# First FFN's second product: the order of the next layer's leading weights, the tails and the first steps' splits

## The chip, the cores and the metric

The kernel runs on one core of a Trainium2 chip, as one launch. The metric is the device time of one execution in microseconds (us), the median of several executions. Engines are named as in the profile: PE is TensorE, DVE is VectorE, ACT is ScalarE, POOL is GpSimd, and SP is the engine that sends nearly all DMAs.

## The reference

Two layers (DEPTH = 2) work on 512 tokens of width 1024. Layer 0 mixes tokens by a short gated convolution, layer 1 by a Mamba-2 scan; behind each mixer stands a SwiGLU feed-forward network (FFN) with an inner width of 2816. Around each of the four sub-layers stand two RMS norms and a shift, scale and gate that come from a conditioning vector:

```python
h = rmsnorm(x, norm_g[i, 2]) * (1.0 + scale) + shift
gate_, up = jnp.split(h @ f_w_in[i], 2, axis=-1)
y = (jax.nn.silu(gate_) * up) @ f_w_out[i]
x = x + gate * rmsnorm(y, norm_g[i, 3])
...
h = rmsnorm(x, norm_g[i, 0]) * (1.0 + scale) + shift    # next layer
z, xbc, dt_raw = jnp.split(h @ m_w_in, ..., axis=-1)
```

The change is in layer 0's FFN, at the product with `f_w_out[0]`, and in the passage from there to the first product of layer 1, with `m_w_in`. All of it is float32.

## The kernel before

**Split operands.** A float32 matrix product is made of three TensorE products. Each operand is split into a high part (a cast on ScalarE) and a low part (a subtraction on VectorE); `split_w` does this for weights. So each weight tile costs a DMA, one ScalarE and one VectorE instruction, in this order, before TensorE can use it.

**The second product.** The product with `f_w_out[0]` is computed over the first 16 of 22 blocks of the inner width by a Strassen scheme with seven products on quarter matrices (`PRODUCTS`: banks A to D, weights b11 to b22, activations a11 to s1). The list `seq` holds its 28 steps of 12 matmuls ("s") and four plain steps ("p") for blocks 16 and 17 of both column halves and 18 and 19 of half 0; the steps are numbered q = 0 to 31. `w_prep(item)` splits a step's weights, `a_prep(item)` its activations (and updates the raw activations for later products). In the loop, the program of step q holds the product, then `behind(q)` (copies of finished banks, and sums of weight quarters), then `w_prep` of step q + 4 and `a_prep` of step q + 3. The loop of the first product, ahead of it, already splits steps 0 and 1 within its last two tiles. Between the two loops stand the gating of the last inner block (`up(NF - 1, ...)`), the low parts that are still due (`low_parts`), two gate rows and step 2's and step 3's splits.

**Gate rows.** `put_gates(s)` turns a column of gate values into a row: a transpose on TensorE, then (second step of the generator) a copy on VectorE into the tile `gr`, of which there is one, and a DMA on SP to `gate_d`. Rows 2 and 3 are made here; they are read in layer 1.

**Weight rows.** `y_load` brings six tiles of the right half of `f_w_out[0]` (`w2y`) into the places of the activations `h`, which the last tile of the first product reads; two more are in staging buffers (`w4`, `w2s`). `add_` sends sums of weight quarters as accumulating DMAs on Pool.

**Tails and leading weights.** What is left is kept for the end (`tails`: three pieces of two blocks, one for column half 0 and two for half 1), so that the row tiles of 128 tokens end one after the other. Their raw weights are loaded into `xns`, tiles that later take the normalized rows, and that lie where `wx` lay. For the first product of layer 1, six weight tiles are prepared ahead (`ssd_lead`: three loads of 256 columns, `load_lead`; the first has 32 columns of dt and a memset behind them). Each load goes to one of two staging buffers `wst`; the four splits of a load are put into the list `lead_ops`, and the buffer is free for the next but one load when they are done. Load 2 so takes load 0's buffer.

**The boundary.** `finish(tail_w, leads)` runs the order in the string `BOUNDARY`, written out by hand: for each row tile t, the tail's matmuls (m0_t for column half 0, m1a_t and m1b_t for half 1), the bank's sum with the held product and its square (sq0_t, sq1_t; line 432 and 433), the gate (yg, 439), the new x (x, 456), its square (xs, 475) and root (rt3, 485), the normalized row (xn, 493 and 495). Then follow the transposes of row tiles 0 and 1 (tr0_p, line 502), for each block j of h the value (u), the high (hi) and the low part (lo; lines 511 to 520), and the first six tiles of layer 1's product in pieces by k (k0_k for tokens 0 to 255, k1_k for the rest).

Within these parts the order on TensorE, ScalarE, VectorE, SP and Pool is the program's (`manual_schedule`); each engine works through its instructions in order, and each waits for its operands.

Of the kernel before, what the change touches and what calls it, by code (L numbers as in the profile page):

```python
# [9 lines left out]
F32R = mybir.dt.float32r  # L10
# [6 lines left out]
P = 128  # L17
T = 512
# [20 lines left out]
def trunk_kernel(  # L39
# [17 lines left out]
    whl_p = ctx.enter_context(tc.tile_pool(name="whl", bufs=4))  # L57
# [147 lines left out]
    def split_w(src, dst, nk):  # L205
        act.copy(dst[:, 0, :nk, :], src)
        dve.tensor_tensor(dst[:, 1, :nk, :], src, dst[:, 0, :nk, :].bitcast(F32), SUB)
# [102 lines left out]
    def put_gates(s, bank=aux_ps):  # L310

        pt = bank("ggp")
        pe.transpose(pt[:KD, :P], gcol[:, s * KD:(s + 1) * KD], ident)
        yield
        gr = tmp.tile([KD, P], F32, tag="gr", name="gr", bufs=1)
        dve.tensor_copy(gr, pt[:KD, :P])
        dma(gate_d[s], gr)
        yield
# [261 lines left out]
    with ExitStack() as ph:  # L580
# [113 lines left out]
        with tc.manual_schedule(engines={PE_ENGINE, mybir.EngineType.SP, mybir.EngineType.Activation,  # L694
# [7 lines left out]
            load = lead_load(0, 1)  # L702
# [207 lines left out]
            for k in range(18):  # L910
                i, jp = k % 6, 2 + k // 6 * 2
# [65 lines left out]
        def tile4l(shape, dtype, name):  # L977
            return lead_p[0].tile(shape, dtype, tag="b", name=name)
# [30 lines left out]
        def up(f, pst):  # L1009
            g = gates[f]  # L1010
            if f < NS:
                dve.tensor_mul(raw[f // 4][:, f % 4, :], pst, g)
                if f % 4 == 3:
                    p = f // 2 - 1
                    lows.append(lambda: dve.tensor_tensor(a_("s1", p, 2), a_("a21", p, 2), a_("a22", p, 2), SUB))
                    lows.append(lambda: dve.tensor_tensor(a_("a21", p, 2), a_("a11", p, 2), a_("a21", p, 2), SUB))
                return
            a = acts[f] = ffp.tile([P, 2, T], F32R, tag="a", name=f"ff{f}")
            dve.tensor_mul(g, pst, g)
            act.copy(a[:, 0, :], g)  # L1020
            lows.append(lambda: dve.tensor_tensor(a[:, 1, :], g, a[:, 0, :].bitcast(F32), SUB))

        def low_parts():
            while lows:
                lows.pop(0)()
# [75 lines left out]
        def a_prep(item):  # L1101
            if item[0] == "p":
                return
            a = a_of[item] = ao_p[0].tile([P, 2, 2, 256], F32R, tag="ao", name="ao")
            (i, p), _ = tiles_s[item[1]]
            src = a_(PRODUCTS[i][2], p, 2)
            act.copy(a[:, 0], src)
            dve.tensor_tensor(a[:, 1], src, a[:, 0].bitcast(F32), SUB)
            if i == 0:
                dve.tensor_tensor(a_("a11", p, 2), a_("s1", p, 2), a_("a11", p, 2), SUB)  # L1110
            elif i == 1:
                dve.tensor_add(a_("a12", p, 2), a_("a12", p, 2), a_("a11", p, 2))
# [39 lines left out]
        with tc.manual_schedule(engines={PE_ENGINE, mybir.EngineType.SP, mybir.EngineType.Activation,  # L1152
                                         mybir.EngineType.DVE, mybir.EngineType.Pool}):
            load_pair(0)
            madds = ada_begin(14)
            for i, f in ((0, 0), (2, 0), (1, 1), (3, 1), (4, 2), (5, 3)):
                rest(i)
                if i in (2, 3):
                    up(f, lead_ps[i])
                    sums(1)  # L1160
                    low_parts()
                else:
                    gate(f, lead_ps[i])
                sums(1)
            finish = out_begin(1, w2, lambda k: acts[k], NF, ggs, xn_lead, "aux", None,
                               lambda: load_w([(wm_in, P, P)]), ys=ys, held=held)[2]
            plain_tiles = finish(())
            tiles = []
            last = 2 * NF - 7
            for k in range(last + 1):  # L1170
                if k % 2 == 0 and k < 2 * NF - 10:
                    load_pair(k // 2 + 1)
                if k in (16, 20, 24):
                    x_load((k - 16) // 4)
                if k in (last - 2, last - 1):
                    xy_load(n_s - 2 + k - last + 2)
                tiles.append(in_chunk(ws[k], h))
                for step in todo:
                    next(step, None)
                q, j = divmod(k - 3, 4)  # L1180
                if j < 2 and k > 2:
                    gate(4 + 2 * q + j, tiles[k - 1])
                elif k:
                    up(2 + 2 * q + j, tiles[k - 1])
                if k + 2 < len(splits):
                    for op in splits[k + 2]:
                        op()
                low_parts()
                sums(4 if j < 2 else 3)
                if k == 2 * NF - 12:  # L1190
                    ggs.append(make_gg(1, gg_tile))
                if k == last - 1:
                    assert next(madds, None) is None and not ada_sets and not quarters
                    sums_p.close()
                    ph.enter_context(tc.tile_pool(name="gap", bufs=1, side="right", reuse_waits="tile")).tile(
                        [P, 216], F32, tag="gap", name="gap")
                    ao_p.append(ph.enter_context(tc.tile_pool(name="aop", bufs=3, side="right", reuse_waits="tile")))
                    ao_p[0].tile([P, 2, 2, 256], F32R, tag="ao", name="ao")
                    gotp = ph.enter_context(tc.tile_pool(name="gotp", bufs=1, side="right", reuse_waits="tile"))
                    c22 = gotp.tile([P, 2, T], F32, tag="c22", name="c22")  # L1200
                if k >= last - 1:
                    w_prep(seq[k - last + 1])
                    a_prep(seq[k - last + 1])
            up(NF - 1, tiles[-1])
            low_parts()
            for step in todo:
                list(step)
            for q in (2, 3):
                list(put_gates(q, mm_ps))
            for p in range(n_s - 2):  # L1210
                y_load(p)
            for p in range(n_s):
                add_(b_("b12", p), b_("b11", p))
            w_prep(seq[2])
            w_prep(seq[3])
            a_prep(seq[2])
            leads, lead_ops, tail_w = [], [], [[], []]
            tails = ((0, NF - 2), (1, NF - 4), (1, NF - 2))
            for q, item in enumerate(seq):
                if item[0] == "s":  # L1220
                    product(item)
                else:
                    w = w_of[item]
                    plain_tiles(item[1], [(item[2] + kk, w, kk) for kk in range(2)], item[3])
                behind(q)
                if q == 13:
                    plain[1, NS] = plain_load(1, NS, flat_half(s1t, 0))
                    plain[0, NS] = plain_load(0, NS, flat_half(s1t, 1))
                elif q == 24:
                    plain[0, NS + 2] = plain_load(0, NS + 2, flat_half(wx[0], 0))  # L1230
                if q + 4 < len(seq):
                    w_prep(seq[q + 4])
                if q + 3 < len(seq):
                    a_prep(seq[q + 3])
                if q == 27:
                    st_p.close()
                    lead_p.append(ph.enter_context(tc.tile_pool(name="leadp", bufs=16, reuse_waits="tile")))
                    xns += [tile4l([P, 2, T], F32, "xn") for _ in range(4)]
                    for xn, (hf, k0) in zip(xns, tails):
                        plain[hf, k0] = plain_load(hf, k0, xn)  # L1240
                    for load in ssd_lead[:2]:
                        leads += load(lead_ops)
                if q >= 28:
                    if q - 28 < len(tails):
                        hf, k0 = tails[q - 28]
                        w = whl_p.tile([P, 2, 2, T], F32R, tag="whl", name="whlo")
                        split_w(plain[hf, k0], w, 2)
                        tail_w[hf] += [(k0 + kk, w, kk) for kk in range(2)]
                    for op in lead_ops[3 * (q - 28):3 * (q - 27)]:
                        op()  # L1250
                    if q == 29:
                        leads += ssd_lead[2](lead_ops)
            for op in lead_ops[12:]:
                op()
            begun = finish(tail_w, leads)
        h, lead_ps, rest, wz1 = begun

# [1056 lines left out]
```

## Time and profile before

| | |
|---|---|
| time, three runs | 1337.48 to 1338.66 us, median 1337.7 |
| the profiled execution | 1338.2 us; span of the profile 1336.4 us; mean granted TensorE clock 0.996 |
| busy over the span | PE 1316.8 us (99%), DVE 1028.1 (77%), ACT 641.9 (48%), POOL 85.9 (6%) |
| the second product, q = 0 to 31 | 450.63 to 544.3 us of the span |
| row tiles of the boundary | 544.3 to 560 us |
| first transposes of the rows | 566.19 us |

Times in the text are microseconds from the span's start. The timeline's rows give start, duration, engine, line, operation, output and inputs, shapes, count, and in brackets the idle time of the engine just before and what ended it. The names `cA` to `cD` are banks, `whlo` a split weight tile, `ao` a split activation tile, `li` the first tiles of layer 1. Matmuls overlap: each is shown with its whole latency.

### The profile page before, as it was taken

The numbers are of one execution on the slowest core, as the hardware profiler recorded it, in microseconds if no ns is written. First come the engines' busy times: TensorE is split into PE (matmuls) and PEld (weight loads), VectorE is DVE, ScalarE is ACT, GpSimd is POOL, SyncE is SP. The second block draws the span as 40 slices with busy tenths as digits, with TensorE's granted clock in tenths as the row PEclk, the third lists the DMA queues.
The fourth block names the chain that finished last, engine by engine and source line by source line (L and its number), as shares of the span: only waits on it lengthen the run. The fifth ranks groups of instructions, "written<-read, shape, count | busy, mean of one in ns | idle before, by whom it ended". The sixth has DMA issues, their size and how long they took to land.

```text
span 1336.4 us, 19228 instructions
## 1 busy us (share of the span) xinstructions
PE 1316.8 (99%) x7437; PEld 1136.7 (85%) x7437; DVE 1028.1 (77%) x1654; ACT 641.9 (48%) x1042; POOL 85.9 (6%) x106
## 2 busy tenths in 40 slices
PE   8999999999999999899999999999999999999997
PEld 7788889888888788698888888888789999998886
DVE  5588866788676696658899889888687777766887
ACT  5323256212122565655654555554474455544665
POOL 0000000000000050000000000000000111101320
PEclk9999999999999999999999999999999999999999
DMA  9767760788885492513542434323251888868861
GB/s 308 237 183 229 249 217 1 228 274 247 290 290 181 137 193 53 157 33 115 158 141 83 124 112 141 113 93 111 95 158 37 193 210 216 206 180 288 180 124 64
DMA packets 203456, 222.21 MB, mean 166 GB/s; under 512 B 8788, under 2 KB 148964, under 8 KB 202340
## 3 DMA queue, kind: packets, MB, share of 16 engines
q1 hardware_dynamic: 186496, 184.74, 44.7%
q0 software_dynamic: 12720, 23.34, 10.1%
q10 hardware_dynamic: 4148, 12.90, 3.0%
q8 instruction: 58, 0.95, 0.3%
q14 instruction: 34, 0.28, 0.1%
HBM read 195.37 MB, written 2.24 MB: 148 GB/s over the span
## 4 chain that ended last, share of the span: by engine, by line
PE 93%; DVE 2%; DMA 2%; ACT 1%; issue 1%; SPq 0%; DVEq 0%; ACTq 0%
PE ip L279 14%; PE ip L281 14%; PE ip L280 14%; PE y L381 10%; PE sA L1904 7%; PE cA L1999 4%; PE sC L1904 3%; PE li L279 3%; PE li L280 3%; PE li L281 3%; PE cA L1127 2%; PE li L767 2%; PE sB L1904 2%; PE yd L1496 1%; PE cD L1999 1%; PE cC L1999 1%
## 5 line engine op out<-in xcount | busy, mean ns | idle before, releaser
L279 PE MATMUL ip<-h,whl 128*128 128x512 f32 x840 | 331.2, 394 | 0.2 <-DVE cv L874 0.2
L281 PE MATMUL ip<-h,whl 128*128 128x512 f32 x840 | 327.2, 389 | 0.0
L280 PE MATMUL ip<-h,whl 128*128 128x512 f32 x840 | 327.0, 389 | 0.0
L279 PEld LDWEIGHTS ip<-h,whl 128*128 128x128 f32 x840 | 157.8, 188 | 33.8 <-issue 1.8
L281 PEld LDWEIGHTS ip<-h,whl 128*128 128x128 f32 x840 | 157.7, 188 | 33.3
L280 PEld LDWEIGHTS ip<-h,whl 128*128 128x128 f32 x840 | 157.8, 188 | 31.6
L225 DVE TENSOR_TENSOR whl<-wst,whl 128x1024 fp32r<-128x1024 f32 x99 | 120.4, 1221 | 41.4 <-ACT whl L224 41.3
L224 ACT CAST whl<-wst 128x1024 fp32r<-128x1024 f32 x99 | 102.4, 1042 | 62.8 <-DMA wst<-in_f_w_in_dram 59.1
L127 DVE SCALAR_TENSOR_TENSOR ada_acc<-ada_st,csil,ada_acc 128x512 f32<-128x512 f32 x140 | 105.0, 750 | 22.1 <-DMA ada_st<-in_ada_w_dram 18.8
L381 PE MATMUL y<-whlo,ys 128*128 128x512 f32 x384 | 89.4, 392 | 0.0
L381 PEld LDWEIGHTS y<-whlo,ys 128*128 128x128 f32 x384 | 71.7, 188 | 15.9 <-issue 0.7
L279 PE MATMUL li<-h,whl 128*128 128x256 f32 x288 | 83.4, 290 | 0.0
L280 PE MATMUL li<-h,whl 128*128 128x256 f32 x288 | 81.6, 283 | 0.0
L281 PE MATMUL li<-h,whl 128*128 128x256 f32 x288 | 81.6, 283 | 0.0
L1904 PE MATMUL sA<-tq,whl 128*128 128x256 f32 x576 | 74.6, 283 | 0.3 <-DVE g L1930 0.3
L1904 PEld LDWEIGHTS sA<-tq,whl 128*128 128x128 f32 x576 | 71.6, 192 | 0.6 <-DVE g L1930 0.5
L1350 DVE SCALAR_TENSOR_TENSOR cu<-ip,cols,cu 128x511 f32<-128x511 f32 (+2 forms) x84 | 62.7, 747 | 4.0 <-ACT cu L1347 1.4
L1999 PE MATMUL cA<-whlo,ao 128*128 128x512 f32 x264 | 61.2, 391 | 0.8 <-DVE ao L1978 0.4
L1999 PEld LDWEIGHTS cA<-whlo,ao 128*128 128x128 f32 x264 | 49.3, 188 | 12.2 <-ACT whlo L1964 1.2
L1860 DVE TENSOR_TENSOR whl<-wsu,whl 128x1024 fp32r<-128x1024 f32 x33 | 40.4, 1223 | 23.4 <-ACT whl L1859 23.4
L279 PEld LDWEIGHTS li<-h,whl 128*128 128x128 f32 x288 | 55.4, 192 | 0.0
L280 PEld LDWEIGHTS li<-h,whl 128*128 128x128 f32 x288 | 55.3, 192 | 0.0
(371 smaller groups left out, 2324.2 us busy)
## 6 DMA issues: line engine op xcount, KB each, us to landing
ada_st<-in_ada_w_dram SPq DMA_DIRECT2D x96, 512.0 KB, 5.7
wst<-in_f_w_in_dram SPq DMA_DIRECT2D x26, 1024.0 KB, 7.6
wst<-in_m_w_in_dram SPq DMA_DIRECT2D x14, 1024.0 KB, 5.4
wst<-in_m_w_in_dram SPq DMA_DIRECT2D x20, 512.0 KB, 4.1
wst<-in_a_w_in_dram SPq DMA_DIRECT2D x9, 1024.0 KB, 6.7
wsu<-in_f_w_in_dram SPq DMA_DIRECT2D x17, 512.0 KB, 5.4
csb<-cs_d ACTq DMA_DIRECT2D x8, 1024.0 KB, 6.6
sg<-in_f_w_in_dram SPq DMA_DIRECT2D x32, 256.0 KB, 3.4
```

What stands on the lines that cost most here:

```text
L127: dve.scalar_tensor_tensor(acc, w, csil[:, k:k + 1], acc, MUL, ADD)
L224: later.append((lambda sw=sw, w=w: act.copy(w[:, 0, :nk, :], sw), lambda sw=sw, w=w: dve.tensor_tensor(w[:, 1, :nk, :], sw, w[:, 0, :nk, : ...
L225: lambda sw=sw, w=w: dve.tensor_tensor(w[:, 1, :nk, :], sw, w[:, 0, :nk, :].bitcast(F32), SUB)))
L279: pe.matmul(dst, w_at(w, 0, kk), a[:, 0, sl], start=start, stop=False)
L280: pe.matmul(dst, w_at(w, 0, kk), a[:, 1, sl], start=False, stop=False)
L281: pe.matmul(dst, w_at(w, 1, kk), a[:, 0, sl], start=False, stop=stop)
L381: pe.matmul(pst, a[:, al, tk], wt[:, wl, kk, :], start=k == 0 and i == 0, stop=k == K - 1 and i == 2, skip_group_check=bool(held))
L767: pe.matmul(acc_of(i), w[:, part // 2, k, c0:c0 + P], h[kk][:, part % 2, :], start=(kk, part) == (0, 0), stop=(kk, part) == (KD - 1, 2))
L1350: dve.scalar_tensor_tensor(u[:, sft:], pst[:, :T - sft], w[3 - sft], u[:, sft:], MUL, ADD)
L1860: dve.tensor_tensor(dst[:, 1], src, dst[:, 0].bitcast(F32), SUB)
L1904: pe.matmul(dst, w[:, wl, k0 + k, :], moving(q, k, al), skip_group_check=True, start=q in ("P1", "P5", "P2") and k == 0 and i == 0, stop=k ...
L1999: pe.matmul(bank[r][sub], a[:, al, q, tk], w[:, hl, q, :], start=first and k == 0, stop=last and k == 2, skip_group_check=True)
```

## The change

Nothing is computed otherwise; instructions are moved.

At the start, w_prep and a_prep of step 2 are put behind those of step 1, ahead of the last gating. The low part of the last inner block is made behind step 3's weights. The gate rows' transposes stay ahead of product 0; their copies and DMAs go behind `behind(0)` and `behind(1)`, so that the y loads and the accumulating DMAs precede them in the program.

At the end, the loads 0 and 1 of the leading weights are sent ahead of the tails' loads. The splits of load 0 stand in step 27, ahead of all tails, and load 2 is sent there. The splits of load 1 are around the first tail's split in step 28, the second and third tails' splits in steps 29 and 30, and load 2's splits behind the third tail's (two in step 30, two in step 31).

```diff
+            w_prep(seq[2])
+            a_prep(seq[2])
             up(NF - 1, tiles[-1])
-            low_parts()
             for step in todo:
                 list(step)
-            for q in (2, 3):
-                list(put_gates(q, mm_ps))
+            rows_g = [put_gates(q, mm_ps) for q in (2, 3)]
+            for step in rows_g:
+                next(step)
             for p in range(n_s - 2):
                 y_load(p)
             for p in range(n_s):
                 add_(b_("b12", p), b_("b11", p))
-            w_prep(seq[2])
             w_prep(seq[3])
-            a_prep(seq[2])
+            low_parts()
...
+            def tail_split(i):
+                hf, k0 = tails[i]
+                w = whl_p.tile([P, 2, 2, T], F32R, tag="whl", name="whlo")
+                split_w(plain[hf, k0], w, 2)
+                tail_w[hf] += [(k0 + kk, w, kk) for kk in range(2)]
...
                 behind(q)
+                if q < 2:
+                    list(rows_g[q])
...
                     xns += [tile4l([P, 2, T], F32, "xn") for _ in range(4)]
+                    for load in ssd_lead[:2]:
+                        leads += load(lead_ops)
                     for xn, (hf, k0) in zip(xns, tails):
                         plain[hf, k0] = plain_load(hf, k0, xn)
-                    for load in ssd_lead[:2]:
-                        leads += load(lead_ops)
-                if q >= 28:
-                    if q - 28 < len(tails):
-                        hf, k0 = tails[q - 28]
-                        w = whl_p.tile([P, 2, 2, T], F32R, tag="whl", name="whlo")
-                        split_w(plain[hf, k0], w, 2)
-                        tail_w[hf] += [(k0 + kk, w, kk) for kk in range(2)]
-                    for op in lead_ops[3 * (q - 28):3 * (q - 27)]:
+                    for op in lead_ops[:4]:
                         op()
-                    if q == 29:
-                        leads += ssd_lead[2](lead_ops)
-            for op in lead_ops[12:]:
-                op()
+                    leads += ssd_lead[2](lead_ops)
+                elif q == 28:
+                    for op in lead_ops[4:6]:
+                        op()
+                    tail_split(0)
+                    for op in lead_ops[6:8]:
+                        op()
+                elif q == 29:
+                    tail_split(1)
+                elif q == 30:
+                    tail_split(2)
+                    for op in lead_ops[8:10]:
+                        op()
+                elif q == 31:
+                    for op in lead_ops[10:]:
+                        op()
             begun = finish(tail_w, leads)
```

## The prediction

> **What bounds the kernel now.** I began with the engine shares of the profile page, then took TensorE's timeline around the first FFN's second product, then the chain of waits in order of time, and last the single queues that feed its two holes.
>
> ```profile
> PE 1316.8 (99%) x7437; PEld 1136.7 (85%) x7437; DVE 1028.1 (77%) x1654; ACT 641.9 (48%) x1042; POOL 85.9 (6%) x106
> ```
>
> TensorE is the bound (99% of the span): only a hole in its stream can move the end, and time that it gains here is kept if nothing later waits. The holes near the change, in its timeline (start, duration, what, idle before it):
>
> ```profile
> 450.63 6.15 PE L1127 MATMUL cA<-whlo,ao 128*128 128x512 f32 x26
> 457.59 5.30 PE L1127 MATMUL cA<-whlo,ao 128*128 128x512 f32 x22 [0.80 <-DVE ao L1108]
> ...
> 545.69 1.75 PE L381 MATMUL cC<-whlo,ff 128*128 128x512 f32 x7
> 547.83 1.43 PE L381 MATMUL cC<-whlo,ff 128*128 128x512 f32 x5 [0.39 <-DVE whlo L207]
> ...
> 550.46 2.88 PE L381 MATMUL cC<-whlo,ff 128*128 128x512 f32 x12
> ...
> 558.62 1.52 PE L381 MATMUL cD<-whlo,ff 128*128 128x512 f32 x6
> 566.19 1.51 PE L502 MATMUL xtr<-ident,xn 128*128 128x128 f32 x4 [6.05 <-ACT xn L493]
> 567.36 2.91 PE L381 MATMUL cD<-whlo,ff 128*128 128x512 f32 x6
> ```
>
> A matmul of 512 columns ends 0.39 us after its start, but the next one starts earlier: the twelve at 550.46 start every (2.88 - 0.39) / 11 = 0.227 us. So what a hole costs is counted from start to start. First hole: 457.59 - 450.63 - 26 x 0.227 = 1.06 us. Second: 547.83 - 545.69 - 7 x 0.227 = 0.55. Third: TensorE is free at 558.62 + 6 x 0.227 = 559.98 and goes on at 566.19, 6.21 us later. Behind it the six matmuls at 567.36 take 2.91 instead of 1.52. The windows name the cause (length, busy time and count of PE, PEld, DVE, ACT, POOL, then the granted clock):
>
> ```profile
> 560.20:566.10 5.90, 0.00 (x0) 0.00 (x0) 5.10 (x14) 4.60 (x16) 0.00 (x0) 0.87 0.00 0
> 566.20:570.70 4.50, 4.36 (x14) 3.38 (x15) 1.76 (x4) 3.70 (x9) 0.00 (x0) 0.50 0.00 2
> ```
>
> After some 4.5 us without matmuls the clock falls to half and stays there while the next matmuls run. The third hole therefore costs more than its length. What fills it, in the chain of waits:
>
> ```profile
> 532.50 9.43 DMA wst<-in_m_w_in_dram
> ...
> 545.88 5.45 DMA wst<-in_m_w_in_dram
> 551.35 0.63 ACT whl L206
> 552.00 1.29 DVE whl L207 x2
> 553.30 0.61 DVE c L432
> ```
>
> VectorE is held by the last split of the next layer's leading weights until 553.3, because their last load lands at 551.3. Only then comes the first step on row tile 0 (sq0_0, line 432), whose matmuls ended 7 us earlier. The rows' norm chain then has no wait for TensorE: it is late as a whole.
>
> **Part 1, first steps.** The first hole is the low part of step 2's activations. Ahead of it on VectorE:
>
> ```profile
> 452.98 1.22 DMA gate_d<-gr
> 454.53 2.41 DVE whlo L1099 x3
> 456.93 0.61 DVE ao L1108
> ```
>
> ```profile
> 454.32 0.28 DVE L316 COPY gr<-ggp 8x128 f32<-8x128 f32 x1 [1.36 <-DMA gate_d<-gr]
> ```
>
> Both gate rows share one small tile, so the second copy waits 1.36 us for the first one's DMA. The change puts w_prep and a_prep of step 2 ahead of all that (and of the last gating), and the copies behind products 0 and 1. Even if only the 1.36 us went, the split would come 1.36 earlier against a hole of 1.06; steps 3 and 4 move up with it, as VectorE still has the same splits to do, less a wait. The two ggp transposes stay where they are. The last FFN tile's low part (0.69) goes behind step 3's splits; its first reader is a tail 90 us later: nothing. Gain 1.06.
>
> Each moved instruction has a DMA on SP: the y loads are now ahead of both gate rows. What is then queued:
>
> ```profile
> 454.96 3.18 SPq L1056 DMA_DIRECT2D w2y<-in_f_w_out_dram  x6
> ```
>
> ```profile
> w2y<-in_f_w_out_dram SPq DMA_DIRECT2D x6, 512.0 KB, 6.5
> ```
>
> The y loads wait only for the last tile's reads of h. In the second FFN the like loads leave one by one while the last tile still runs: first at 1218.46, TensorE's product at 1223.02.
>
> ```profile
> 1218.46 4.41 SPq L1784 DMA_DIRECT2D w2h<-in_f_w_out_dram  x4
> ```
>
> ```profile
> 1223.02 1.29 PE L1999 MATMUL cA<-whlo,ao 128*128 128x512 f32 x5
> ```
>
> By that distance (4.56) they leave from about 446 here (450.6 less 4.56), not 454.96, and with 6.5 us median landing are about done when gate row 0 is sent. Its copy stands behind step 3's weight splits; those end at 454.53 + 2.41 = 456.9 now, and I take the same time. Row 1's copy comes one step's VectorE work later (2.41 / 2 for the weights, 0.61 and as much again for the activations and their update, about 2.4), at 459.3, and a row landing 1.22 after 456.9 keeps nothing waiting. If the y loads left only at 450.6 the row would land some 4 us later: VectorE would wait 2 to 3 us, and TensorE at step 4 about 2 of them. I take zero; the other end stays in the range. The Trainium skill speaks here (DMA: Bandwidth & Descriptors, Queues, rings and completion order): on each DMA engine the descriptors of a queue are consumed in order, so 4 KB behind 3 MB pays for the 3 MB. By it alone the row would be no earlier than the y loads, which is the same rival as below. In this trace the row's 1.22 us has nothing ahead of it, so no row here tests it.
>
> **Part 2, leading weights ahead of the tails.** The staging buffers of loads 0 and 1 are free when the last step's weights are split:
>
> ```profile
> 523.43 1.30 DVE L1099 TENSOR_TENSOR whlo<-w2s,whlo 128x512 fp32r<-128x512 f32 x2
> ```
>
> that is at 524.7. SP now sends their four DMAs then, not behind the tails (first lead DMA waited for above: sent 532.50). The tails can't leave earlier than now (their buffer is the one of the last plain step), so they lose only what of the leads is still in flight.
>
> ```profile
> 533.00:545.00 12.00, 12.00 (x54) 9.95 (x53) 4.60 (x6) 5.19 (x8) 0.00 (x0) 1.00 0.89 251
> ```
>
> At 251 GB/s: the leads' first 1.7 MB take 6.8 us, landing at about 532.5; three tails (1.57 MB) at about 539; load 2 (1.05 MB) at about 543, since its buffer is free when the first four splits are through (after the last plain split and the memset, about 534). From landing to the end of its splits took 552.00 + 1.29 - 551.35 = 1.94 before. So VectorE is free at about 545. Nothing on TensorE waits for ScalarE or VectorE in this stretch (steps 28 to 31 are split before), and the tails land 5 us before their first use (545.69 - 6 x 0.227 = 544.3). The second hole goes: +0.55.
>
> Now sq0_0 is bound by TensorE: tile 0 of column half 0 ends at 545.46 + 0.39 = 545.9. Half 1 of tile 0 ends with the twelfth matmul from 545.69, with no hole: 545.69 + 11 x 0.227 + 0.39 = 548.6. From there the chain runs as it does now:
>
> ```profile
> 555.42 0.68 DVE L432 TENSOR_TENSOR c<-cC,c 128x512 f32<-128x512 f32 x1
> ```
>
> ```profile
> 565.43 1.32 ACT L493 ACTIVATE xn<-x,ss 128x512 f32<-128x512 f32 x2
> ```
>
> 555.42 becomes 548.6, 6.8 earlier, and so do the row-1 steps (their matmuls are done 1 us or more before they are needed). The first transpose, 566.19, is ready at 559.4; TensorE comes at 559.98 - 0.55 = 559.43. The second transpose needs the second xn: (565.43 + 1.32) - 6.8 = 559.95, a wait of 0.4. The third hole is gone, and with it the half clock. What TensorE does from the hole to the third transpose group:
>
> ```profile
> 572.93 0.60 PE L502 MATMUL xtr<-ident,xn 128*128 128x128 f32 x4
> 573.28 0.36 PE L279 MATMUL li<-h,whl 128*128 128x256 f32 x1
> ...
> 575.15 0.38 PE L502 MATMUL xtr<-ident,xn 128*128 128x128 f32 x2
> ```
>
> At full clock: transposes 0.35, six matmuls 1.36, transposes 0.35, fifteen matmuls for k = 0 as those for k = 1, 575.15 - 573.28 = 1.87: 3.93 us. Now it takes 572.93 - 559.98 = 12.95. Left over after the change: 0.4 for the second xn and about 0.2 for h's low part, which takes 1.47 us behind the transposes against 1.71 of TensorE's work, but starts behind ScalarE's square of tile 2:
>
> ```profile
> 567.74 0.56 ACT L513 ACTIVATE u<-xtr,mods,acol 128x256 f32<-128x256 f32 x1
> ```
>
> ```profile
> 568.78 0.43 DVE L520 TENSOR_TENSOR h<-u,h 128x256 fp32r<-128x256 f32 x1 [0.46 <-ACT h L516]
> ```
>
> Gain 12.95 - 3.93 - 0.6 = 8.4. Of it about 2.6 is the clock. The Trainium skill (TensorE: Matmul & The Clock Gate, Part 1) gives a warm-up of about 3.4 us, so at half speed about 1.7 lost, 0.9 less than I take. This trace has 0.50 over 566.20 to 570.70 alone, already longer; the trace decides.
>
> **Sum.** 1.06 + 0.55 + 8.4 = 10.0 us. The profiled execution took 1338.2 (span 1336.4), 0.5 over the median of the runs, 1337.7. So 1328.2 for it, and 1327.7 for the median.
>
> **Rivals.** (a) The leads land too late: what decides is load 2. Each us behind 544 delays sq0_0, and beyond 0.7 us of slack opens the hole again by as much. If SP sends the leads only at 530.5 (a buffer held longer than I read), all 4.3 MB land at about 548.5, VectorE is free at 550.5, 4 us after its slack: 1331.5 to 1332, and the clock may fall again. Against: the staging row above. (b) Gate row 1 waits for the y loads: 1 to 3 us, 1329 to 1331. (c) The same wait taken to its end, slower than before: if row 0 lands only when the y loads and the additions that Pool sends behind them are through, VectorE stands at the second copy with the splits of steps 4 and 5 behind it, and TensorE with it. TensorE needs step 4's low part at 450.63 + 50 x 0.227 = 462.0, and it is 0.28 + 1.2 + 0.61 = 2.1 us of VectorE work behind the copy; a landing at 469 stalls 9 us and drops the clock, eating all 10: 1339. It decides from a landing of about 468 on, 11 us after sending; now it takes 1.22. (d) It doesn't do what it says: VectorE stays held to 553 by something other than the splits, and only the first hole goes or not even that: 1337. Against: line 432 starts within 0.1 us of the last split.
>
> **How the numbers follow.** Forecast 0.74, its own range 1326.6 to 1329.6 (the leftover waits at zero and 0.5 for one execution against the next; 1.9 more of waits than I take). (a) 0.11, (b) 0.07, (c) 0.04, (d) 0.04. The range 1326.6 to 1332.0 takes in (a) and (b). About 0.2% (2.7 us) is what a measurement of this kernel can tell from no change. Faster 0.92, same 0.04, slower 0.04.
>
> **What would show it.** Right: no idle of TensorE at about 456 and 547, the first transposes within 1 us of the matmuls before them, granted clock 1.00 from there on, lead DMAs sent at about 524, line 432 right behind TensorE's tile 0. Wrong: a wait for gate_d's DMA on VectorE at 459 with an idle TensorE at 462; splits of in_m_w_in behind 546; a new wait behind k = 0 (the tiles' banks, or the low parts), since VectorE's lead over TensorE there is small.

## The result, and the profile after

The changed kernel takes 1331.57 us (median of five runs, 1330.65 to 1332.37), the kernel before beside it 1337.7 (1337.22 to 1338.66). The ratio is 0.9952, with a 95% interval of 0.9938 to 0.9967: faster by 6.1 us, where 10.0 were forecast. The profiled execution took 1330.71 (span 1328.9, clock 0.999).

TensorE's timeline of the kernel after, at the first steps of the second product (start, duration, what, and in brackets the idle time before it):

```profile
451.09 11.14 PE L1127 MATMUL cA<-whlo,ao 128*128 128x512 f32 x48
462.07 0.61 PE L1127 MATMUL cB<-whlo,ao 128*128 128x512 f32 x2
464.43 10.72 PE L1127 MATMUL cB<-whlo,ao 128*128 128x512 f32 x46 [1.75 <-DVE ao L1108]
```

The hole in step 2 is gone: 48 matmuls run through. A new one stands in step 4, after its first two matmuls. From start to start it costs 464.43 - 462.07 - 2 x 0.227 = 1.91 us. What VectorE did ahead of it, in its own timeline:

```profile
456.69 0.27 DVE L316 COPY gr<-ggp 8x128 f32<-8x128 f32 x1
...
458.73 0.69 DVE L1110 TENSOR_TENSOR raw<-s1t,raw 128x512 f32<-128x512 f32 x1
462.36 0.28 DVE L316 COPY gr<-ggp 8x128 f32<-8x128 f32 x1 [2.94 <-DMA gate_d<-gr]
462.57 1.20 DVE L1099 TENSOR_TENSOR whlo<-w2x,whlo 128x1024 fp32r<-128x1024 f32 x1
463.70 0.67 DVE L1108 TENSOR_TENSOR ao<-raw,ao 128x512 fp32r<-128x512 f32 x1
```

Gate row 1's copy waits 2.94 us for row 0's DMA. Behind it stand the split of step 5's weights and the low part of step 4's activations (463.70), and TensorE waits for the second. Row 0 was sent at 457.0 (SyncE's queue) and landed at 462.3: 5.3 us, not 1.22.

```profile
446.39 3.77 SPq L1056 DMA_DIRECT2D w2y<-in_f_w_out_dram  x6
456.99 5.97 SPq L317 DMA_DIRECT2D gate_d<-gr  x2
```

The y loads did leave at 446, as forecast. How long they took, in the answers on their line, before and then after:

```profile
DMA to landing us min/median/max: 4.0/6.5/12.2
```

```profile
DMA to landing us min/median/max: 6.4/9.2/12.4
```

Pool's additions wait for the y loads. Its first one in Pool's timeline, before and then after:

```profile
459.61 1.00 POOL L1046 DMA_DIRECT2D w2y<-w2x  x1 [456.46 <-DMA w2y<-in_f_w_out_dram]
```

```profile
450.84 1.00 POOL L1046 DMA_DIRECT2D w2y<-w2x  x1 [447.68 <-DMA w2y<-in_f_w_out_dram]
```

At the boundary, TensorE's timeline of the kernel after:

```profile
547.07 2.88 PE L381 MATMUL cC<-whlo,ff 128*128 128x512 f32 x12
...
559.31 1.52 PE L381 MATMUL cD<-whlo,ff 128*128 128x512 f32 x6
560.78 0.33 PE L502 MATMUL xtr<-ident,xn 128*128 128x128 f32 x1
561.39 0.55 PE L502 MATMUL xtr<-ident,xn 128*128 128x128 f32 x3 [0.28 <-ACT xn L493]
561.69 1.64 PE L381 MATMUL cD<-whlo,ff 128*128 128x512 f32 x6
...
565.39 0.60 PE L502 MATMUL xtr<-ident,xn 128*128 128x128 f32 x4
```

The second and the third hole are gone. TensorE is free at 559.31 + 1.36 = 560.67 and reaches the third group of transposes at 565.39: 4.72 us where it took 12.95. VectorE's timeline shows why:

```profile
544.90 1.29 DVE L207 TENSOR_TENSOR whl<-wst,whl 128x512 fp32r<-128x512 f32 x2 [0.42 <-ACT whl L206]
547.27 0.69 DVE L432 TENSOR_TENSOR c<-cB,c 128x512 f32<-128x512 f32 x1 [1.07 <-PE cB L381]
549.99 0.69 DVE L432 TENSOR_TENSOR c<-cC,c 128x512 f32<-128x512 f32 x1 [0.43 <-PE cC L381]
```

The last split of the leading weights ends at 546.2 instead of 553.3, and row tile 0's first steps now wait for TensorE, not TensorE's next work for them.

**The two profiled executions, added up.** 1.06 (step 2) + 0.55 (the second hole, at the third tail) + 8.23 (12.95 - 4.72) - 1.91 (step 4) - 0.45 (this execution is that much later already where the change begins: its gate transposes come at 450.95 against 450.50) = 7.48 us. Measured: 1338.2 - 1330.71 = 7.49. Nothing is left over in this pair; that the median is 0.9 above this execution is taken up below.

### The profile page after: what moved, and what is told of

Same layout as the page of the kernel before. It is cut to its first block, busy times and chain, and to the rows that moved or that the text cites. A ratio compares the mean times of both kernels' runs of the same rounds, so it can differ in the third digit from the quotient of the medians.

```text
span 1328.9 us, 19226 instructions
## 1 busy us (share of the span) xinstructions
PE 1314.1 (99%) x7437; PEld 1134.3 (85%) x7437; DVE 1028.2 (77%) x1654; ACT 641.7 (48%) x1042; POOL 86.1 (6%) x106
## 4 chain that ended last, share of the span: by engine, by line
PE 94%; SPq 2%; DVE 2%; ACT 1%; DMA 1%; issue 1%; DVEq 0%; ACTq 0%
PE ip L279 15%; PE ip L281 14%; PE ip L280 14%; PE y L381 10%; PE sA L1920 7%; PE cA L2015 4%; PE sC L1920 3%; PE cA L1127 3%; PE li L279 3%; PE li L281 3%; PE li L280 3%; PE sB L1920 2%; PE li L767 1%; PE yd L1512 1%; PE cC L2015 1%; PE cB L2015 1%
## 5 line engine op out<-in xcount | busy, mean ns | idle before, releaser
L2015 PEld LDWEIGHTS cA<-whlo,ao 128*128 128x128 f32 x264 | 49.3, 188 | 12.2 <-ACT whlo L1980 1.2
```

Source lines behind the costliest of these rows:

```text
L2015: pe.matmul(bank[r][sub], a[:, al, q, tk], w[:, hl, q, :], start=first and k == 0, stop=last and k == 2, skip_group_check=True)
```

## The experiments

Three theories were set against each other. Q: gate row 0 stands behind the y loads in SyncE's DMA queue, and row 1's copy, step 4's activations behind it and TensorE wait for it. S: it isn't the queue but the 16 DMA engines, shared with the y loads and the accumulating DMAs (the additions that Pool sends), that keep the row. U: the start brings its 1.06, and the loss lies elsewhere. Each kernel was timed in five rounds beside the kernel before; times are medians, with the ratio to before and its interval.

**The start alone** (`e1_start_only`): the change without its part at the end.

> Only the change at the start (step 2's splits ahead, the gate rows' copies behind products 0 and 1); the end as before. Theory Q (gate row 0 stands behind the y loads in SP's DMA queue, row 1's copy waits for it on VectorE, TensorE at step 4 for VectorE): the hole of 1.06 us at step 2 goes, one of about 1.9 at step 4 comes: 0.9 slower than before, 1338.6. Theory U (the start gives its 1.06 and what is missing from the forecast is lost at the boundary or behind it): 1336.6.

Measured: 1339.72, ratio 1.0014 (1.0005 to 1.0023): the start by itself makes the kernel slower. TensorE's timeline, and then the windows around the hole (length, busy time and count of PE, PEld, DVE, ACT, POOL, then granted clock, DMA share, GB/s):

```profile
461.68 0.61 PE L1127 MATMUL cB<-whlo,ao 128*128 128x512 f32 x2
464.19 12.30 PE L1127 MATMUL cB<-whlo,ao 128*128 128x512 f32 x46 [1.90 <-DVE ao L1108]
```

```profile
462.00:464.30 2.30, 0.40 (x3) 0.11 (x1) 2.14 (x4) 2.02 (x4) 1.74 (x2) 1.00 0.88 155
464.30:467.70 3.40, 3.40 (x9) 2.62 (x10) 3.37 (x5) 0.00 (x0) 0.87 (x1) 0.50 1.04 175
467.70:476.00 8.30, 8.30 (x38) 6.89 (x37) 7.96 (x14) 5.00 (x9) 3.48 (x4) 1.00 0.55 93
```

The same hole, and here the clock falls to half for 3.4 us behind it: the 46 matmuls take 12.30 us instead of 10.72, 1.6 more. So the new wait cost 1.9 us in the kernel after, and here, where the clock falls, 2.06 (464.19 - 461.68 - 2 x 0.227) + 1.58 = 3.6 us; the 0.9 expected by Q had left the clock out. U is out.

**The end alone** (`e2_end_only`): the change without its part at the start.

> Only the change at the end (leading weights loaded and split ahead of the tails); the start as before, with its hole at step 2. Theory Q: 0.55 + 8.2 = 8.8 off, 1328.9, faster than the whole change. Theory U: the whole change's 6.1 less 1.06, that is 5.1 off, 1332.6.

Measured: 1329.5, ratio 0.9936 (0.9923 to 0.9948), 2 us better than the whole change. The passage to layer 1 brings 8.6 us of the 8.9 to 9.0 forecast for it (0.55 + 8.4).

**Both rows' copies later** (`e3_rows_late`): the whole change, but the copies behind products 6 and 9.

```diff
-                if q < 2:
-                    list(rows_g[q])
+                if q in (6, 9):
+                    list(rows_g[q // 9])
```

> The whole change, but the gate rows' copies and DMAs stand behind products 6 and 9, when the y loads have landed. Theory Q: no hole at step 2 and none at step 4, all of the forecast: 1327.9, about 1 below the end alone. Theory U: as the whole change, 1331.6. VectorE has 0.26 us of slack for each step there and the copy takes 0.2, so a hole of up to 0.3 at step 7 would agree with both.

Measured: 1328.42, ratio 0.9927 (0.9914 to 0.9941): 9.8 us faster than before. TensorE's timeline has no hole at all in the first steps:

```profile
450.59 11.14 PE L1127 MATMUL cA<-whlo,ao 128*128 128x512 f32 x48
461.57 11.04 PE L1127 MATMUL cB<-whlo,ao 128*128 128x512 f32 x48
```

**Both rows in one copy** (`e8_one_row_copy`): the whole change, with one transpose of both rows' columns, one copy of 16 rows behind product 0 and one DMA of 8 KB. The y loads ahead of the transfer land as late as before (the slowest after 12.5 us), but no second copy waits for its buffer.

```diff
+            pt_g = mm_ps("ggp")
+            pe.transpose(pt_g[:2 * KD, :P], gcol[:, 2 * KD:4 * KD], ident)
...
+                if q == 0:
+                    gr = tmp.tile([2 * KD, P], F32, tag="gr", name="gr", bufs=1)
+                    dve.tensor_copy(gr, pt_g[:2 * KD, :P])
+                    dma(gate_d[2:4].rearrange("s j p -> (s j) p"), gr)
```

> The whole change, but both gate rows in one: one transpose of 16 columns, one copy behind product 0, one DMA of 8 KB. The DMA traffic is as in the whole change, but nothing on VectorE waits for a gate row. If that wait (2.94 us, one small tile for two rows) is the whole loss: no hole at step 4, 1328.4 as with the rows late. If the traffic or the earlier accumulating DMAs cost something by themselves: 1329.5 to 1331.

Measured: 1328.57, ratio 0.993 (0.9918 to 0.9943), and no hole (48 matmuls from 462.23 in 11.04 us). Taken away in two ways, by place and by buffer, the wait gives back the same 3 us. So, within the intervals, it is the whole loss.

**The rows on ScalarE's queue** (`e4_rows_act_queue`): this tells Q from S, since that queue holds nothing else then.

```diff
-        dma(gate_d[s], gr)
+        (dma_s if s > 1 else dma)(gate_d[s], gr)
```

> The whole change, but the two gate rows' DMAs are sent by ScalarE, on its own queue, at the same place in the program. Theory Q (order in SP's queue): row 0 lands 1 to 2 us after its copy, VectorE waits less than 0.5, no hole at step 4: 1327.9 to 1328.5. Rival S (the shared DMA engines are full of y loads and accumulating DMAs, whatever the queue): the wait stays at 2 to 3 us, 1330.5 to 1331.6.

Measured: 1330.65, ratio 0.9946 (0.9934 to 0.9959): little gained on the whole change. ScalarE's timeline and VectorE's:

```profile
456.38 0.29 ACTq L317 DMA_DIRECT2D gate_d<-gr  x1
...
461.60 1.05 ACT L1098 CAST whlo<-w2x 128x1024 fp32r<-128x1024 f32 x1 [3.26 <-DVE gr L316]
```

```profile
460.91 0.28 DVE L316 COPY gr<-ggp 8x128 f32<-8x128 f32 x1 [0.51 <-DMA gate_d<-gr]
```

Sent at 456.4 into a queue of its own, the row still lands only at 460.9: 4.5 us. In the trace its 16 packets move only from 459.5 on. Until then, from 456.3, its queue moves none, while Pool's queue moves 279 (86% of the engines' time) and SyncE's 150. Q as stated, with the order in the queue as the whole cause, falls. Moreover ScalarE now stands for 3.26 us with the next split behind its own DMA, so the wait has only changed its engine; the run bears on the row's time, not on what the kernel could reach.

**The additions later** (`e10_adds_later`): the whole change, with a small copy on Pool that reads step 3's split weights put ahead of the accumulating DMAs. It holds them back from 450.8 to 456.7. Beside it on the same chip ran **the change once more** (`e11_change_again`).

```diff
-            for p in range(n_s):
-                add_(b_("b12", p), b_("b11", p))
             w_prep(seq[3])
             low_parts()
+            pool.tensor_copy(small(1), w_of[seq[3]][:, 1, 1, 0:1].bitcast(F32))
+            for p in range(n_s):
+                add_(b_("b12", p), b_("b11", p))
```

> The whole change, with a small GpSimd copy that reads step 3's split weights put ahead of the accumulating DMAs, so that these are sent from about 456 us on instead of 450.8. If it is their packets, from 455 us on, that hold gate row 0 back on the shared DMA engines, the row lands near 458, VectorE doesn't wait for it, and the time is 1328.0 to 1328.6, as with the rows put later. If the y loads alone hold the row, VectorE still waits some 3 us and the time is about 1331.

> The change as it is, on the same chip as the two others of this call. From its first five times: 1330.7 to 1332.4, some 3 us above the versions in which nothing waits for the gate rows. If the clock stays full behind the hole at step 4 the execution is near 1330.7, if it falls to half for 3.4 us, near 1332.4.

Measured: 1328.85, ratio 0.9932 (0.9918 to 0.9945), against 1331.01, ratio 0.9949 (0.9937 to 0.9962). With the additions later, Pool's timeline, the landing of the y loads, and VectorE's second copy:

```profile
456.72 2.80 POOL L1046 DMA_DIRECT2D w2y<-w2x  x3
```

```profile
DMA to landing us min/median/max: 6.5/7.8/8.4
```

```profile
459.19 0.27 DVE L316 COPY gr<-ggp 8x128 f32<-8x128 f32 x1
```

The slowest y load lands after 8.4 us, not 12.4; row 0 is sent at 456.9, as in the kernel after, and is through by 459.2, so its successor doesn't wait. The additions that Pool sent from 450.8 on were what made the y loads, and the row with them, late. The queue windows agree: from 444 to 458 us the kernel after moves this on Pool's queue, and the one with the additions later nothing.

```profile
q0 software_dynamic: 139, 0.27, 10.3%
```

The profiled execution of the repeat is one in which the clock falls. Its 46 matmuls show it against 10.72 above, and its windows give the place (the granted clock is the third number from the end):

```profile
464.53 12.35 PE L1127 MATMUL cB<-whlo,ao 128*128 128x512 f32 x46 [1.92 <-DVE ao L1108]
```

```profile
464.50:465.00 0.50, 0.47 (x2) 0.43 (x3) 0.49 (x1) 0.00 (x0) 0.10 (x1) 1.00 1.14 197
465.00:465.50 0.50, 0.50 (x4) 0.41 (x3) 0.50 (x2) 0.00 (x0) 0.49 (x1) 1.00 1.14 188
465.50:466.00 0.50, 0.50 (x3) 0.41 (x3) 0.50 (x1) 0.00 (x0) 0.38 (x1) 0.88 0.84 135
466.00:467.00 1.00, 1.00 (x4) 0.71 (x4) 0.96 (x3) 0.00 (x0) 0.00 (x0) 0.50 1.09 186
...
468.50:469.00 0.50, 0.50 (x2) 0.40 (x2) 0.50 (x2) 0.50 (x2) 0.00 (x0) 0.50 0.32 49
```

It took 1332.47, the execution profiled first 1330.71. Such a fall in some executions and not in others can make up 1.8 of the 3.0 us of the change's spread (1329.6 to 1332.6 over the ten runs) and would put its median above the execution profiled first; only these two were profiled.

**The passage, edit by edit.** What brings the 8.6 us, the sending order or the order of the splits? In the kernel before, loads 0 and 1 were sent ahead of the tails with the splits left as they were (`e6_loads_first`); in the end alone, the loads were put back behind the tails (`e7_splits_order`; the diff is the first one's, the second has these lines the other way round).

```diff
+                    for load in ssd_lead[:2]:
+                        leads += load(lead_ops)
                     for xn, (hf, k0) in zip(xns, tails):
                         plain[hf, k0] = plain_load(hf, k0, xn)
-                    for load in ssd_lead[:2]:
-                        leads += load(lead_ops)
```

> The kernel before with one edit at the end: the loads 0 and 1 are sent ahead of the tails' loads, the splits stay in their old order (each tail ahead of three lead splits), so load 2 is sent in step 29. The start is as before. If the sending order is what counts: load 2 is sent at about 540.5, lands at about 546.5, VectorE is free at about 548.3, 1.6 us late: 1331.1 against 1329.5 of the whole end. If the order of the splits counts as much: most of the hole stays, 1335 or more.

> The new order of the splits with the old order of the loads (tails first); the start as before. The first four splits now wait for load 0, which lands behind the tails at about 542, and the tails' splits stand behind them: the first tail's weights are ready at about 546.5 instead of 537.3, TensorE waits about 2 us at 544.3, and the rows' chain starts at about 551.6. So 1337 to 1339, no gain by the splits alone. If the splits' order were the cause of the gain: near 1329.5.

Measured: 1333.59, ratio 0.9969 (0.9958 to 0.9981), and 1337.06, ratio 0.9993 (0.9984 to 1.0002). The sending order alone brings about half, the new order of the splits alone nothing that can be told; together they bring twice the first. TensorE's timeline of the loads first and what held it, on ScalarE:

```profile
562.38 0.33 PE L502 MATMUL xtr<-ident,xn 128*128 128x128 f32 x1 [2.51 <-ACT xn L493]
```

```profile
545.82 1.14 ACT L206 CAST whl<-wst 128x512 fp32r<-128x512 f32 x2 [2.94 <-DMA wst<-in_m_w_in_dram]
```

Load 2 is sent only when load 0's splits are through (541.6, against 536.0 in the kernel after), lands 3.3 us later than there, and leaves a hole of 2.5 us with half the clock behind it for 3.4 us. So the time lies between the two that were expected: VectorE reached line 432 at 549.4 instead of 548.3, and a fall of the clock had not been counted.

**The price of the half clock** (`e5_warm`, `e9_warm_short`): the kernel before, with filler matmuls of the identity put ahead of the first transposes, where TensorE waits anyway; 50 of them in the first, 24 in the second.

```diff
                 pt = self.pt[hi, p] = mk[0]("xtr")
+                for _ in range(24 if s == 1 and (hi, p) == (0, 0) else 0):
+                    pe.matmul(pt[:, :P], ident, ident, start=True, stop=True)
```

> The kernel before, with 50 idle matmuls of the identity (128 columns, about 0.11 us each, 5.5 us together) into the bank of the first transposes, just ahead of them: TensorE does them while it waits for the rows, so the hole's 6.2 us stay, but the clock need not fall. If the half clock cost what I took (2.6): 1335.6 against 1338.2. By a warm-up of 3.4 us as the rule has it (1.7): 1336.5. If it cost nothing that the rows' chain would not cost anyway: 1338.2.

> The kernel before with 24 filler matmuls ahead of the first transposes of the boundary; the transpose wait itself stays. In the run with 50 of them each issued as two of 0.112 us, so 24 take 5.4 us and lie inside the 6.2 us in which TensorE stands idle. What is tested is the price of the half clock behind that idle stretch alone. If the half clock costs the 2.6 us of the prediction's sum: 1337.9 - 2.6 = 1335.3. If it costs what 3.4 us at half clock lose: 1337.9 - 1.7 = 1336.2. If it costs nothing: 1337.9.

Measured: 1340.79, ratio 1.0022 (1.0013 to 1.0031), and 1336.23, ratio 0.9988 (0.9979 to 0.9996). The first missed, by its own size: each filler issues as two matmuls, and 50 of them overfill the 6.2 us. The second fits. TensorE's timelines of the two:

```profile
560.69 11.32 PE L500 MATMUL xtr<-ident 128*128 128x128 f32 x100
```

```profile
561.06 5.52 PE L500 MATMUL xtr<-ident 128*128 128x128 f32 x48
567.20 0.33 PE L504 MATMUL xtr<-ident,xn 128*128 128x128 f32 x1 [0.62 <-ACT xn L493]
...
568.12 1.62 PE L381 MATMUL cD<-whlo,ff 128*128 128x512 f32 x6
...
571.81 0.60 PE L504 MATMUL xtr<-ident,xn 128*128 128x128 f32 x4
```

From the first transposes to the third group 4.61 us pass instead of 572.93 - 566.19 = 6.74: the half clock cost 2.1 us net. This stretch is read from one execution, the slowest of the eleven (1338.2). By the times of all it is 1.6 (0.5 to 2.8). The 1.7 and the 2.6 of the expectation both lie in that interval; the times don't decide between them.

## Why the prediction was right, and where it wasn't

The time fell in the range, on the forecast side, but 3.9 us short of the forecast and outside the forecast's own range (1326.6 to 1329.6). What happened is rival (b), whose times ended at 1331; that the range reaches 1332.0 comes from rival (a), which did not happen. So the last 0.6 us were luck.

- **First hole, 1.06:** right; the 48 matmuls run through.
- **Gate row 1's wait, taken at zero:** the step that failed. The y loads did leave at 446.39 and the second copy was due at 459.4 (458.73 + 0.69; 459.3 forecast), but "about done" went by their median landing of 6.5 us. The slowest decides, and the same answer on the kernel before has it at 12.2. And an edit that sends the loads 8.6 us earlier lets Pool's additions, which wait for them, go earlier too: at 450.84 instead of 459.61, straight into the y loads and the row. The prediction followed SyncE's queue past the move, and Pool's only in the rival that ended slower. Its other bound, 2 to 3 us on VectorE and about 2 on TensorE, is what came: 2.94 and 1.91. That is rival (b) (1329 to 1331, chance 0.07), which left out that the clock falls behind such a hole in some executions, for 1.6 more. The Trainium skill's rule (DMA: Bandwidth & Descriptors, Queues, rings and completion order) that a queue's descriptors are consumed in order pointed the right way, but the row on an empty queue shows that it isn't the whole: 4.5 us there against 5.3. Another sentence of that section of the Trainium skill is that an engine takes turns between the queues that have work for it, a packet at a time. The row on its own queue doesn't bear that out: it moved no packet until 459.5, while Pool's and SyncE's queues moved 429.
- **Second hole, 0.55:** right; no idle time stands in the tail's matmuls at 547.07.
- **Leading weights:** sent at 525.5 (524 forecast), load 2 in ScalarE's hands at 542.5 and 544.2 (543), VectorE free at 546.2 (545), 1.07 us ahead of TensorE. Rival (a) did not come. It is near, though: with the splits of load 0 left late, load 2 comes 3.3 us later and (a) is there.
- **Third hole and clock, 8.4:** 8.23 measured. The 0.4 us for the second normalized row is there as 0.28 of idle time. The 2.6 of the clock and the leftover waits meet in this: the half clock had hidden that wait, so 2.1 is its net price. The Trainium skill (TensorE: Matmul & The Clock Gate, Part 1) gives windows of about 3.4 us; the 3.4 us at 0.50 in the start alone agree. In the kernel before it was longer, by its windows from about 564.6 to 571.4 (granted clock 0.79 from 564 to 565, 0.50 up to 571, 0.80 from 571 to 572).
- **The sum:** without the wait for the row, the change brings 9.8 us (7.9 to 11.5, rows late) or 9.4 (7.6 to 11.0, one copy): the 10.0 of the sum.

Open is how much of the row's 5.3 us is order in its queue and how much is shared engines. Behind the y loads it landed 0.1 us after the last of them (sent at 449.8, landed 12.4 us later, at 462.2); on a queue of its own it landed 0.7 us ahead of it (460.9 against 449.2 + 12.4 = 461.6). The later additions shorten both: the y loads ahead of it are through sooner, and the engines are freer. Why the row's own queue moved nothing for 3 us isn't shown.

Why the clock falls in one execution and not in the next behind a hole of about 2 us was not tested either. The hole that left it full was the shortest (1.91 us from start to start, against 2.06 and 2.09 in the start alone and the repeat), so the length may decide, or the moment at which the hole falls. The Trainium skill (TensorE: Matmul & The Clock Gate, Part 1) has the clock's window running freely, which would fit the second. It has the fall behind an idle window of about 3.4 us; these holes were shorter, and here the measurement decides.

## What to carry to other kernels

When an instruction is moved, follow every queue whose head it releases: here earlier loads freed Pool's additions too, and these slowed a transfer of 4 KB that VectorE waited for. Judge a transfer by the slowest landing of what shares its engines, not by the median or by how it lands in a quiet stretch, and give a small tile that is refilled behind a DMA room for both contents, or put its refill where the DMAs are through. Send loads in the order in which their data are used, and place the splits so that the staging buffer of the next load comes free: either alone brought half or nothing.

## What the runs showed that was not expected

The granted clock falls behind holes much shorter than the 6.2 us of the kernel before: with 1.90, 1.92 and 2.51 us of idle time it fell for 3.4 us, with 1.75 it stayed. In the repeat it was still 1.00 in the first us after TensorE had gone on, and fell only then. So a stall of 2 us cost 3.6 in one execution.

A row of 4 KB sent into a queue of its own took 4.5 us while other queues kept the DMA engines busy, 3 of them before its first packet, and 1.22 in a quiet stretch. And a float32 matmul of the identity issues as two matmuls of 0.11 us, which doubled the filler.
